# Norm factor in PSUM for VectorE, two weight pairs loaded early into idle gate-output slots, weight loads held for the u stores, and a new order of stages, in an eight-core convolutional decoder

## Chip, cores, metric

One Trainium2 chip, a program on all 8 cores. The time is the device time of the slowest core, in microseconds (us). Executions fall into a fast and a slow state (in the slow one a die runs longer at a lower granted clock); only fast runs are compared here. "Profiled core" is the slowest core of the profiled run; where a number is a median over the eight cores of a trace, the text says so.

## The reference

Two layers, each with an RMSNorm, one input projection, a Conformer convolution branch (A), a short gated convolution branch (B), one output projection and a residual add; a last RMSNorm gives the output. Cut to what matters:

```python
def rmsnorm(x, g):
    xf = x.astype(jnp.float32)
    xn = xf * lax.rsqrt(jnp.mean(xf * xf, axis=-1, keepdims=True) + RMS_EPS)
    return xn.astype(x.dtype) * g
...
    h = rmsnorm(x, norm_g)
    p = jnp.einsum('btd,de->bte', h, w_in)                           # (B, T, D_IN)
...
    u = a_val * jax.nn.sigmoid(a_gate)                               # GLU
    ca, new_a = causal_dwconv(u, buf_a, conv_a_w)
    ca = head_layernorm(ca + conv_a_b, ln_a_g, ln_a_b)
    y_a = jax.nn.silu(ca) * jax.nn.silu(z_a)
    v = gc * hb
    cb, new_b = causal_dwconv(v, buf_b, conv_b_w)
    y_b = gb * cb * jax.nn.silu(z_b)
    y = jnp.einsum('bte,ed->btd', jnp.concatenate([y_a, y_b], axis=-1), w_out)
    return x + y, new_a, new_b
...   # trunk: both layers, then
    return rmsnorm(x, final_g), jnp.stack(new_as, axis=0), jnp.stack(new_bs, axis=0)
```

Each core has one prompt of 2048 tokens and 64 sample tokens, in blocks of 512, 512, 512, 512 and 64 columns.

## The kernel before

The kernel records operations with their data dependences and lets its own list scheduler put them in order on each engine. A stage is a token of the order string: P = one pair of GLU projections (u), C = one convolution, a and b = short-convolution projections, Z = the gate path of A, O4 = a round of the output projection over four finished gate outputs. The second string is the second layer's. Of the transfers, the u stores (`su0`, `su1`) write a finished u to DRAM, and `up` reads it back in the layout that the convolution needs; `toep` holds the weights of a convolution as VectorE lays them out.

```python
ORDER = [
    "b0 C0 Z0 P2 C1 a1 b1 P3 C2 P4 Z1 O4 C3 P5 a2 Z2 b2 Z3 C4 a3 P6 b3 O4 C5 Z4 P7 a4 b4 C6 Z5 a5 b5 C7 Z6 a6 b6u0 a7 Z7u1 b7up",
    "b0 C0 Z0 P2 C1 a1 b1 P3 C2 P4 Z1 O4 C3 P5 a2 Z2 b2 Z3 C4 a3 P6 b3 C5 Z4 P7 O4 a4 b4 C6 Z5 a5 b5 C7 Z6 a6 b6u0 a7 Z7u1 b7up",
]
...
    def rms_stat(part, fill=None, fill_n=(), pool=False, after=(), early=False):
        q, off, n = part
        b = V("bank", "stat")
        ...   # ScalarE squares two chunks, VectorE or GpSimd adds, TensorE sums with a ones matrix into bank b
        r = V("tmp")
        ...
        lo = act((lambda e: e.activation(out=tm(r, n), in_=bank(b, n), func=AF.Ln, bias=RMS_EPS)), n, [b], [r], tab="ln",
                 name=f"rln{q}")
        ...
        ex = act((lambda e: e.activation(out=tm(r, n), in_=tm(r, n), func=AF.Exp, scale=-0.5)), n, [r], [r], sbuf=True, tab="ln",
                 name=f"rex{q}")
        lo.follow = ex
        return r

    def rms_apply(gcol0, part, r, final=False, shared=()):
        ...
            if k in shared:     # final stage only: chunks 2, 5 and 7
                S.op("pool", (lambda e, k=k: e.tensor_tensor(out=xs(k, part), in0=xs(k, part), in1=tm(r, n), op=ALU.mult)), 0.15 + n * 0.0021,
                     [xp(k, part), r], [xp(k, part)], name=f"h{q}.{k}")
            else:               # the "h multiply"
                dve((lambda e, k=k, out=out: e.scalar_tensor_tensor(
                    out=out, in0=xs(k, part), scalar=vecs[:, gcol0 + k:gcol0 + k + 1], in1=tm(r, n), op0=ALU.mult, op1=ALU.mult)),
                    n, [xp(k, part), r, vecs_r], [xp(k, part) if final else h_r[k][q]], ptr=1, name=f"h{q}.{k}")
            ...                 # final: store each pair of chunks (SyncE)
```

```python
    # the scheduler: a load issued by GpSimd waits until the "up" transfers in flight are done
                if e == "pool" and o.chan is not None and t > QUIET:
                    small = {x for x in flying if x.done is None}
                    if small:
                        held.setdefault(o, set()).update(small)
                        skipped.append(it)
                        continue
...
            if o.chan in ("up",):
                flying[:] = [x for x in flying if x.done is None] + [o]
...
    # weights: nine slots of 128 x 1024 in wsl; y_sb has five slots for gate outputs
    def proj(w, q, split=1, **kw):
        ...
            pairs = [((lambda k=k: wsl[:, w.slot, k * 128:(k + 1) * 128]), (lambda k=k: hv(k, q))) for k in ks]
...
    # output projection, layer boundary and end: for each part eight output groups, the statistics of that part,
    # and the h multiplies of the part before
        for part in order:
            for m in range(KC):
                out_block(part, m, lhs, ws + tps, ys)
            r = rms_stat(part, pool=part is not order[-1])
            if before:
                rms_apply(gcol0, *before, final, shared)
```

## Time and profile before

Three runs: 1133.47, 1134.51 and 1342.2 us (the last slow); median 1134.51, from which the prediction starts. From the matmul records of all eight cores I cut the span into stretches, each from the start of one named matmul to the start of the next (the last but one to the end of its matmul); medians of the eight cores:

| stretch (us) | before |
|---|---|
| start to last startup statistic | 66.2 |
| on to the first boundary statistic ("first layer") | 455.5 |
| boundary, first to last statistic | 58.2 |
| second layer | 481.3 |
| first statistic of the output to the last projection matmul ("final projection") | 54.2 |
| after the last projection matmul ("tail") | 13.2 |

How to read it: TensorE works almost without a break in the two long stretches, so only the start, the boundary and the end, and single late weights in the first layer, can give time. The profile lines behind this are in the prediction.

### The profile page before, as it was taken

The page shows a single profiled execution, that of the slowest core. Times are in us where ns is not written, and L with a number is a line of the kernel's source. Part 1 is how long each engine was busy: PE and PEld are TensorE (multiplying, and loading weights), DVE is VectorE, ACT ScalarE, POOL GpSimd, SP SyncE. Part 2 cuts the span into 40 slices and gives each one's busy share as a digit, 9 for nine tenths or more (in the row PEclk, how much of TensorE's full clock was granted, in tenths as well). Part 3 has the DMA queues.
Part 4 walks back from the last instruction along what each step waited for, and adds up shares of the span by engine and source line. Part 5 has one row for each costly group of instructions (what it writes and reads, how often), then busy time and mean ns, then how long its engine had stood idle before and what let it go on. Part 6 is the DMA issues. An engine that isn't in the chain of part 4 may idle for free.

```text
span 1133.5 us, 20988 instructions; the slowest of 8 cores (1126.1 to 1133.5 us)
## 1 busy us (share of the span) xinstructions
PE 1094.8 (97%) x7085; PEld 544.0 (48%) x7085; DVE 780.5 (69%) x1576; ACT 445.5 (39%) x704; POOL 272.6 (24%) x418
## 2 busy tenths in 40 slices
PE   5998999999999999999999999999999999999995
PEld 2444545455445455444444455545545445544444
DVE  3773956897677677754774586687876758774577
ACT  4752334324421443543342144333453223553444
POOL 6120212121202121104451122102211111110286
PEclk9999999999999999999999999999999999999998
DMA  9838689558655757661021876856756633564034
GB/s 217 213 69 136 98 140 161 85 83 113 119 86 85 127 80 113 102 103 20 1 42 14 158 138 109 156 94 120 122 92 117 130 52 66 98 95 101 11 132 165
DMA packets 178823, 117.98 MB, mean 104 GB/s; under 512 B 139168, under 2 KB 152352, under 8 KB 178656
## 3 DMA queue, kind: packets, MB, share of 16 engines
q0 software_dynamic: 34352, 54.97, 33.0%
q1 hardware_dynamic: 144224, 61.65, 24.2%
q8 instruction: 59, 0.97, 0.4%
q14 instruction: 44, 0.36, 0.1%
q10 hardware_dynamic: 144, 0.03, 0.0%
HBM read 132.24 MB, written 36.19 MB: 149 GB/s over the span
## 4 chain that ended last, share of the span: by engine, by line
PE 88%; DMA 4%; POOL 3%; DVE 2%; ACT 2%; issue 2%; DVEq 0%; ACTq 0%; POOLq 0%; SPq 0%
PE psb L584 84%; DMA wsl<-w_in_r 2%; PE psb L757 2%; PE psb L759 2%; DVE h_sb L680 1%; DMA big<-scr_c 1%; DMA scr_c<-big 1%; POOL x_sb L677 1%; DVE x_sb L903 1%; POOL tmp L642 0%; POOL tmp L649 0%; ACT tmp L640 0%; ACT tmp L659 0%; ACT tmp L664 0%; ACT L659 0%
## 5 line engine op out<-in xcount | busy, mean ns | idle before, releaser
L584 PE MATMUL psb<-h_sb,wsl 128*128 128x512 bf16 (+1 forms) x4480 | 823.7, 343 | 7.5 <-DMA wsl<-w_in_r 4.7
L584 PEld LDWEIGHTS psb<-h_sb,wsl 128*128 128x128 bf16 x4480 | 373.2, 98 | 414.8 <-issue 17.8
L584 PE MATMUL psb<-y_sb,wsl 128*128 128x512 bf16 (+2 forms) x992 | 187.1, 336 | 2.4 <-DVE x_sb L903 2.4
L903 DVE TENSOR_TENSOR x_sb<-x_sb,psb 128x512 f32<-128x512 f32 (+2 forms) x248 | 135.5, 575 | 43.5 <-PE psb L584 42.4
L575 POOL DMA_DIRECT2D wsl<-w_in_r x112 | 60.4, 548 | 313.5 <-PE psb L584 206.6
L584 PEld LDWEIGHTS psb<-y_sb,wsl 128*128 128x128 bf16 x992 | 85.1, 98 | 88.5 <-issue 2.6
L884 DVE SCALAR_TENSOR_TENSOR tmp<-vbuf,cw_b_sb,tmp 128x512 f32<-128x512 bf16 (+1 forms) x160 | 103.0, 655 | 23.9 <-ACT tmp L881 11.6
L698 DVE SCALAR_TENSOR_TENSOR u_sb<-tmp,psb 128x512 bf16<-128x512 f32 (+1 forms) x80 | 47.2, 591 | 61.0 <-PE psb L584 52.6
L735 DVE COPY toep<-wt_sb 32x512 bf16<-32x512 bf16 x256 | 74.7, 293 | 20.2 <-DMA wt_sb<-wt_d 9.1
L729 POOL DMA_DIRECT2D wt_sb<-wt_d x64 | 35.0, 547 | 218.8 <-DVE toep L735 124.6
L640 ACT ACTIVATE tmp<-x_sb 128x1024 bf16<-128x1024 f32 (+2 forms) x63 | 52.7, 857 | 85.7 <-DVE x_sb L903 70.0
L854 DVE TENSOR_TENSOR vbuf<-psb,tmp 128x512 bf16<-128x512 f32 (+1 forms) x80 | 47.3, 595 | 56.6 <-PE psb L584 55.8
L696 ACT ACTIVATE tmp<-psb 128x512 f32<-128x512 f32 (+1 forms) x80 | 41.4, 522 | 110.1 <-PE psb L584 108.1
L889 ACT ACTIVATE tmp<-psb 128x512 f32<-128x512 f32 (+1 forms) x80 | 41.6, 522 | 105.2 <-PE psb L584 89.3
L838 ACT ACTIVATE tmp<-big,vecs_sb 128x512 f32<-128x512 bf16 (+1 forms) x80 | 55.7, 731 | 53.0 <-DMA big<-scr_c 46.9
L852 ACT ACTIVATE tmp<-psb 128x512 f32<-128x512 f32 (+1 forms) x80 | 41.4, 521 | 87.7 <-PE psb L584 81.9
L881 ACT ACTIVATE tmp<-vbuf,cw_b_sb 128x512 f32<-128x512 bf16 (+1 forms) x80 | 51.2, 643 | 61.6 <-DVE vbuf L854 57.0
L764 DVE TENSOR_TENSOR big<-psb,cbt_sb 128x320 bf16<-128x320 f32 x128 | 62.4, 487 | 16.8 <-PE psb L759 12.6
L891 DVE TENSOR_TENSOR tmp<-psb,tmp 128x512 f32<-128x512 f32 (+1 forms) x80 | 47.0, 594 | 33.6 <-PE psb L584 31.3
L843 ACT ACTIVATE tmp<-psb 128x512 f32<-128x512 f32 (+1 forms) x80 | 40.6, 520 | 72.0 <-PE psb L584 60.7
L680 DVE SCALAR_TENSOR_TENSOR h_sb<-x_sb,vecs_sb,tmp 128x512 bf16<-128x512 f32 (+1 forms) x80 | 54.9, 742 | 19.7 <-ACT tmp L664 19.7
L844 DVE TENSOR_TENSOR y_sb<-tmp 128x512 bf16<-128x512 f32 (+1 forms) x70 | 41.5, 600 | 21.1 <-ACT tmp L843 20.6
(75 smaller groups left out, 893.8 us busy)
## 6 DMA issues: line engine op xcount, KB each, us to landing
wsl<-w_in_r POOLq DMA_DIRECT2D x112, 256.0 KB, 6.7
scr_u<-u_sb SPq DMA_DIRECT2D x16, 768.0 KB, 8.4
up_sb<-scr_u SPq DMA_DIRECT2D x16, 768.0 KB, 8.4
scr_c<-big SPq DMA_DIRECT2D x16, 640.0 KB, 6.7
big<-scr_c SPq DMA_DIRECT2D x16, 640.0 KB, 6.0
wt_sb<-wt_d POOLq DMA_DIRECT2D x64, 128.0 KB, 3.5
x_sb<-x_d POOLq DMA_DIRECT2D x12, 512.0 KB, 20.2
wsl<-w_out_r POOLq DMA_DIRECT2D x24, 256.0 KB, 6.8
```

The costliest lines, as they stand in the source:

```text
L575: return e.dma_start(out=wsl[:, v.slot, :], in_=src)
L584: ins = e.matmul(bank(v, n), lhsT=l_(), rhs=r_(), start=(first and i == 0), stop=(last and i == len(pairs) - 1))
L640: act((lambda e, s=s, kp=kp: e.activation(out=tmph[:, s.slot, 0:2 * n].rearrange("p (k c) -> p k c", k=2), in_=x2(kp, part), func=AF.Square)),
L680: dve((lambda e, k=k, out=out: e.scalar_tensor_tensor(out=out, in0=xs(k, part), scalar=vecs[:, gcol0 + k:gcol0 + k + 1], in1=tm(r, n), op0 ...
L698: dve((lambda e: e.scalar_tensor_tensor(out=u_blk(ub, q), in0=b3(tm(th, n), q), scalar=1.0, in1=b3(bank(bv, n), q), op0=ALU.add, op1=ALU.m ...
L735: dve((lambda e, p=p, c=c: e.tensor_copy(toep[p, tp.slot, :].rearrange("p (m x) -> p m x", x=128)[:, :, 32 * c:32 * c + 32], wt_sb[p, w.sl ...
L764: dve((lambda e, b=b, v=v, bias=bias: e.tensor_tensor(out=big[:, co.slot, 4 * b:4 * b + 4, :], in0=banks[v.slot][:, 0:384].rearrange("p (g ...
L838: act((lambda e, s=s, q=q, n=n: e.activation(out=b3(tm(s, n), q), in_=c_blk(cn.slot, q), func=AF.Silu, scale=vecs[:, 16 + col:17 + col], b ...
L854: dve((lambda e: e.tensor_tensor(out=v_blk(q, 0), in0=b3(bank(bh, n), q), in1=b3(tm(th, n), q), op=ALU.mult)), n, [bh, th], [v_r[q]], name ...
L881: act((lambda e, a=a, q=q, n=n: e.activation(out=b3(tm(a, n), q), in_=v_blk(q, 0), func=AF.Copy, scale=cw_b[:, l, j, 2:3])), n, [v_r[q], c ...
L884: dve((lambda e, a=a, q=q, n=n, lag=lag: e.scalar_tensor_tensor(out=b3(tm(a, n), q), in0=v_blk(q, lag), scalar=cw_b[:, l, j, 2 - lag:3 - l ...
L903: dve((lambda e: e.tensor_tensor(out=xs(m, part), in0=xs(m, part), in1=bank(v, n), op=ALU.add)), n, [v, xr], [xr], name=f"x{q}.{m}")
```

## The change

The intent: (1) VectorE's h multiply reads the norm factor from PSUM and so doesn't share SBUF reads with GpSimd; (2) the weights of P2 and a1 need no weight slot and come early; (3) weight loads stay out of the way of the u stores (`su0` and `su1` in the diff); (4) an order of stages that fits this. A `lock` flag lets the scheduler model the SBUF port that VectorE and GpSimd share (see the prediction); `FIRST` groups the first blocks one by one, which changes nothing. The diff, cut to its core:

```diff
 ORDER = [
-    "b0 C0 Z0 P2 C1 a1 b1 P3 C2 P4 Z1 O4 C3 P5 a2 Z2 b2 Z3 C4 a3 P6 b3 O4 C5 Z4 P7 a4 b4 C6 Z5 a5 b5 C7 Z6 a6 b6u0 a7 Z7u1 b7up",
-    "b0 C0 Z0 P2 C1 a1 b1 P3 C2 P4 Z1 O4 C3 P5 a2 Z2 b2 Z3 C4 a3 P6 b3 C5 Z4 P7 O4 a4 b4 C6 Z5 a5 b5 C7 Z6 a6 b6u0 a7 Z7u1 b7up",
+    "b0 C0 Z0 P2 a1 b1 C1 P3 C2 P4 Z1 O4 C3 P5 a2 Z2 b2 P6 Z3 C4 a3 b3 O4 a4 C5 P7 Z4 C6 b4 Z5 a5 b5 C7 a6 Z6 b6u0 a7 Z7u1 b7up",
+    "b0 C0 Z0 P2 a1 b1 C1 P3 C2 P4 Z1 O4 C3 P5 a2 Z2 b2 P6 Z3 C4 a3 b3 O4 a4 C5 P7 Z4 C6 b4 Z5 a5 b5 C7 a6 Z6 b6u0 a7 Z7u1 b7up",
 ]
+YW = ("P2", "a1")
...
-            if o.chan in ("up",):
+            if o.chan in ("up", "su0", "su1"):
...
+    def w_pair(tok, srcs):
+        if tok not in YW:
+            return [w_load(src) for src in srcs]
+        v = V("y")
+        ws = [YWeight(v, i) for i in range(2)]
+        for w, src in zip(ws, srcs):
+            nload[0] += 1
+            pooldma((lambda e, w=w, src=src: e.dma_start(out=y_sb[:, v.slot, 1024 * w.half:1024 * w.half + 1024], in_=src)),
+                    1.4, (), [w], f"w{nload[0] % 12}", pkt=0.173, holds=[v], name="w", after=gate)
+        return ws
...
-        ex = act((lambda e: e.activation(out=tm(r, n), in_=tm(r, n), func=AF.Exp, scale=-0.5)), n, [r], [r], sbuf=True, tab="ln",
+        ex = act((lambda e: e.activation(out=bank(b, n), in_=tm(r, n), func=AF.Exp, scale=-0.5)), n, [r], [b], sbuf=True, tab="ln",
                  name=f"rex{q}")
         lo.follow = ex
-        return r
+        if copy:
+            ex.follow = act((lambda e: e.activation(out=tm(r, n), in_=tm(r, n), func=AF.Exp, scale=-0.5)), n, [r], [r], sbuf=True, tab="ln",
+                            name=f"rex{q}")
+        return b, r
...
-                    out=out, in0=xs(k, part), scalar=vecs[:, gcol0 + k:gcol0 + k + 1], in1=tm(r, n), op0=ALU.mult, op1=ALU.mult)),
+                    out=out, in0=xs(k, part), scalar=vecs[:, gcol0 + k:gcol0 + k + 1], in1=bank(r, n), op0=ALU.mult, op1=ALU.mult)),
```

## The prediction

> **What bounds the kernel now.** I read the page first: busy shares and the forty slices.
>
> ```profile
> span 1133.5 us, 20988 instructions; the slowest of 8 cores (1126.1 to 1133.5 us)
> ...
> PE 1094.8 (97%) x7085; PEld 544.0 (48%) x7085; DVE 780.5 (69%) x1576; ACT 445.5 (39%) x704; POOL 272.6 (24%) x418
> ```
>
> TensorE has work in flight for 97% of the span, so the change cannot gain more than about 38.7 us (1133.5 - 1094.8), plus whatever TensorE loses inside its busy time to a halved clock. Nothing in the diff removes a matmul. So the question is where those 38.7 us lie. I asked for busy time by stretch; the columns are length, then PE, PEld, DVE, ACT, POOL, granted clock, DMA share and GB/s:
>
> ```profile
> 0.00:60.00 60.00, 45.45 (x236) 21.30 (x237) 33.05 (x67) 37.12 (x46) 23.91 (x40) 0.97 0.87 205
> 60.00:110.00 50.00, 46.41 (x282) 21.88 (x280) 24.66 (x63) 15.46 (x30) 9.35 (x19) 0.97 0.57 106
> 110.00:530.00 420.00, 419.43 (x2789) 209.22 (x2788) 301.78 (x616) 160.71 (x259) 78.78 (x139) 1.00 0.66 103
> 530.00:590.00 60.00, 55.16 (x305) 25.44 (x304) 46.13 (x76) 25.73 (x34) 32.99 (x30) 0.97 0.11 15
> 590.00:1070.00 480.00, 480.00 (x3198) 239.08 (x3197) 326.67 (x687) 176.76 (x294) 84.12 (x155) 1.00 0.56 99
> 1070.00:1134.00 64.00, 48.32 (x284) 27.10 (x281) 48.25 (x72) 29.70 (x44) 43.42 (x37) 0.91 0.36 136
> ```
>
> TensorE idles 14.6 us while the first x blocks arrive, 3.6 us just after, 0.6 us in the whole middle of layer 0, 4.8 us at the boundary of the layers (the output projection with its RMSNorm statistics), nothing in the middle of layer 1, and 15.7 us at the end. A better order in the middles can gain nothing; it can only break something. Next, TensorE's waits, asked for 60 to 520, 520 to 600 and 1060 to 1134 us in turn:
>
> ```profile
> PE psb L584 <- DMA wsl<-w_in_r: 3.6, 1, 3.6
> ...
> PE psb L584 <- POOL tmp L649: 2.4, 2, 2.0
> PE psb L584 <- DVE x_sb L903: 2.4, 2, 2.0
> ...
> PE psb L584 <- DVE tmp L642: 3.9, 3, 3.2
> PE psb L584 <- POOL tmp L649: 3.1, 3, 1.5
> ```
>
> The first is one weight that came late, until 88.9 us. The others are the square sums (L642, L649) and the residual adds (L903), all made on VectorE and GpSimd. Why those are late, the timeline of 546 to 560 us shows: two h multiplies (L680) that cover 3.26 us, while the GpSimd adds run.
>
> ```profile
> 550.56 1.15 POOL L642 TENSOR_TENSOR tmp<-tmp 128x512 bf16<-128x512 bf16 x1 [3.46 <-ACT tmp L640]
> 550.56 3.26 DVE L680 SCALAR_TENSOR_TENSOR h_sb<-x_sb,vecs_sb,tmp 128x512 bf16<-128x512 f32 x2
> 551.85 1.42 POOL L649 TENSOR_TENSOR tmp<-tmp 128x512 bf16<-128x512 bf16 x1
> 553.74 0.67 DVE L903 TENSOR_TENSOR x_sb<-x_sb,psb 128x512 f32<-128x512 f32 x1
> ```
>
> And the groups by shape (busy us, mean ns):
>
> ```profile
> L903 DVE TENSOR_TENSOR x_sb<-x_sb,psb 128x512 f32<-128x512 f32 x184 | 122.3, 683 | 40.2 <-PE psb L584 39.3
> L680 DVE SCALAR_TENSOR_TENSOR h_sb<-x_sb,vecs_sb,tmp 128x512 bf16<-128x512 f32 x64 | 51.6, 858 | 18.0 <-ACT tmp L664 18.0
> L680 DVE SCALAR_TENSOR_TENSOR x_sb<-x_sb,vecs_sb,tmp 128x512 f32<-128x512 f32 x15 | 20.6, 1402 | 2.1 <-ACT tmp L664 2.0
> L680 DVE SCALAR_TENSOR_TENSOR x_sb<-x_sb,vecs_sb,tmp 128x256 f32<-128x256 f32 x10 | 6.7, 726 | 0.9 <-ACT tmp L664 0.9
> ```
>
> L903 has one SBUF input and one from PSUM, and takes 683 ns wherever it stands. L680 has two SBUF inputs and the same size. In the startup, where GpSimd only issues DMAs, eight of them take 5.39 us (0.67 us each), so 4 x 5.4 = 21.6 us of its 51.6 us are there; the 32 at the boundary get the other 30 us, 0.94 us each. In the final stage they take 1.40 us, twice the uncontended time.
>
> **What the Trainium skill says.** "SBUF — State Buffer", section "Who interferes with whom": a VectorE instruction with two SBUF inputs contends with a GpSimd instruction that reads SBUF, and one with at most one SBUF input, outside the two-port modes, does not; the second to issue waits for the whole of the first. The trace agrees: L680 (two) stretches to 1.40 us, L903 (one) stays at 683 ns. "PSUM — Partial Sum Buffer", the text on engine access, allows one tensor input from PSUM per VectorE instruction, which is what the new form has, and says that GpSimd cannot access PSUM; hence the diff's copy of the factor for the multiplies that the final stage gives to GpSimd. "TensorE: Matmul & The Clock Gate", Part 1: after an idle window of some 3.4 us the clock is halved, and recovers after about 3.4 us of work. The trace agrees: after the 3.6 us gap at 85 us the granted clock of 89 to 95 us is 0.74, and after the gaps at 573 us it is 0.61 in 576 to 580 us.
>
> **The change, part by part.**
>
> (1) The factor in PSUM. The exponential now writes the statistics bank and L680 reads it there. I price the new form by L903, 0.68 us, against 0.67 us uncontended: nothing gained or lost at the start. At the boundary 32 x (0.94 - 0.68) = 8 us of VectorE time go. Per block of 512 VectorE then needs 8 adds + 8 multiplies = 16 x 0.68 = 10.9 us against TensorE's 64 x 0.2155 = 13.8 us, so the adds keep up; now they do not (VectorE is busy 5.0 of 5 us in 571 to 576). I expect the 4.8 us of waits there to go, and with them the halved clock behind: the first two groups of eight matmuls take 2.6 and 2.5 us instead of 1.73, 1.6 us together. Sum 6.4 us.
>
> At the end, 15 x (1.40 - 0.68) + 10 x (0.73 - 0.41) = 14 us of VectorE time go (0.41 us is the 256-wide L903). GpSimd's multiplies, up to 1.72 us against 1.27, shorten too. TensorE's waits between 1080 and 1120 us, 0.8 + 0.8 + 1.5 = 3.1 us, should go. Behind TensorE's last projection matmul (ends 1120.3) 13.2 us follow now. Priced without contention: add 0.45, square 0.65, sum 0.3, matmul 0.3, Ln 0.38, Exp 0.42, second Exp for GpSimd 0.42, three GpSimd multiplies 2.3, store about 3.3 (issue and a median landing of 2.4), and 0.1 us for each of eight hand-overs: 9.3 us. So 3.9 us more. Sum 7.0 us. The extra Exp is on an engine that is 39% busy and costs 0.42 us once, counted here.
>
> (2) Early weights. The 3.6 us wait was for the third projection pair (P2), which had no free weight slot before 75.6 us and then flew with five more weights and two u stores (landing 13.5 us median, 6.7 over the run). In the order of the changed kernel the four weights of P2 and a1 are issued in the startup, behind the x loads in the same queue, into idle y slots, some 50 us before use; from 60 to 76 us the DMA engines moved nothing. Gain 3.6 us, plus 6 us x 0.26 = 1.5 us of lost clock in 89 to 95 us. Sum 5.1 us. Layer 1 gets the same, but had no wait there.
>
> (3) Weight loads wait for u stores too. That shortens 16 stores (8.4 us median), whose readers TensorE does not wait for, and delays weight loads by up to as much. Each pair feeds TensorE for 64 x 0.2155 + 16 x 0.03 = 14.3 us, and nine slots hold some four pairs, so such a delay should be hidden. Gain 0, risk 0 to 4 us.
>
> (4) The new order of the stages. The first convolution comes 24 matmuls earlier, and layer 0 becomes like layer 1. No gain to be had; risk 0 to 3 us. The grouping of the first blocks changes nothing, since every group has one block; the lock flag only steers the scheduler.
>
> Sum: 6.4 + 7.0 + 5.1 = 18.5 us, so 1134.5 - 18.5 = 1116.0 with nothing given back. I add 3.5 us for waits that take the place of removed ones, which gives 1119.5 us (-1.3%).
>
> **The rivals.** (a) The statistics wait, not the multiply, sets the boundary: the bank is now held until the multiplies are done, there are two such banks, and the square sums still go through two GpSimd adds (1.15 us each). For it: the PE order still places the second statistics matmul three output groups (5.2 us) behind the block, and add + square + two adds need about 4.4 us; thin. Against: the multiplies end before the bank after next is wanted. Half the gain at boundary and end would go: about 1126. (b) The middles break: a weight held behind a u store, or a convolution that meets its load. For it: the first u stores land only at 85 to 89 us in the trace, and P2's first u must wait for one. Against: without the weights beside them they should land sooner. 1122 to 1127. (c) The trace's waits are all there is and a better start also speeds the rest, giving more than 2% (below 1111.8): it would need 22.7 us, more than my full sum. (d) The early weights delay the x loads: they stand behind them in the queue, so I give it little; 1130.
>
> **Range and chances.** All removed and nothing new is 1116; half given back is 1125. Below 1112 there is little left to take, since the first 14.6 us of startup wait for x. Range 1113 to 1128; faster by over 2% 0.08, within 2% 0.91, slower by over 2% 0.01.
>
> **What would show it.** The h multiply at about 0.68 us at the boundary and in the final stage; no wait of TensorE for a weight after 60 us; boundary waits under 1.5 us; about 9 us behind the last projection matmul; the middles still without waits. It would be wrong if TensorE idles over 3 us in the middles, if the boundary keeps its waits for L649's successor, or if the PSUM form takes clearly more than 0.7 us.

## The result, and the profile after

The changed kernel takes 1122.91 us, the median of four runs (1121.54 to 1123.34), against 1134.33 us, the median of the three fast runs of the kernel before beside it (a fourth was slow). The ratio is 0.9899, 95% interval 0.988 to 0.9919. (A ratio is the mean time of one kernel's fast runs over that of the other's in the same rounds, so it isn't quite the ratio of the quoted medians.)

The head of its page, and the stretches (columns as in the prediction), answer to those of before:

```profile
span 1121.6 us, 20982 instructions; the slowest of 8 cores (1117.3 to 1121.6 us)
...
PE 1091.3 (97%) x7085; PEld 544.6 (49%) x7085; DVE 759.2 (68%) x1576; ACT 444.6 (40%) x709; POOL 265.5 (24%) x418
```

```profile
60.00:110.00 50.00, 49.60 (x343) 24.77 (x343) 32.17 (x81) 17.53 (x35) 9.54 (x19) 1.00 0.50 109
...
530.00:590.00 60.00, 59.83 (x337) 28.20 (x336) 44.57 (x92) 25.57 (x36) 32.63 (x34) 1.00 0.28 40
...
1060.00:1122.00 62.00, 46.54 (x281) 27.21 (x278) 35.21 (x71) 31.47 (x48) 36.53 (x37) 0.90 0.37 140
```

TensorE's idle time after the startup fell from 3.6 to 0.4 us, that of the boundary from 4.8 to 0.2 us, and the granted clock is 1.00 in both. The last stretch still has 15.5 us (62.00 - 46.54). TensorE's waits, asked for 60 to 520, 520 to 600 and 1060 to 1122 us (waited for: us in total, times, longest):

```profile
PE psb L616 <- DVE h_sb L719: 0.4, 1, 0.4
...
PE psb L616 <- DVE x_sb L942: 0.2, 1, 0.2
...
PE psb L616 <- DVE tmp L676: 1.8, 2, 1.1
```

No weight is waited for, and no GpSimd add. Between 600 and 1060 us there is no wait at all. The groups by shape (L942 is the residual add, L903 before; L719 the h multiply, L680 before):

```profile
L942 DVE TENSOR_TENSOR x_sb<-x_sb,psb 128x512 f32<-128x512 f32 x184 | 124.1, 686 | 49.1 <-PE psb L616 48.1
L719 DVE SCALAR_TENSOR_TENSOR h_sb<-x_sb,vecs_sb,psb 128x512 bf16<-128x512 f32 x64 | 44.1, 743 | 13.7 <-ACT psb L699 13.7
L719 DVE SCALAR_TENSOR_TENSOR x_sb<-x_sb,vecs_sb,psb 128x512 f32<-128x512 f32 x15 | 10.7, 743 | 1.9 <-ACT psb L699 1.8
...
L719 DVE SCALAR_TENSOR_TENSOR x_sb<-x_sb,vecs_sb,psb 128x256 f32<-128x256 f32 x10 | 4.2, 475 | 0.8 <-ACT psb L699 0.8
```

The multiply of the final stage fell from 1402 to 743 ns, and that of 128x256 from 726 to 475 ns. At the boundary, the mean of the 32 multiplies of 128x512 fell from 957 to 744 ns, counted one by one in the traces. The timeline of the boundary shows the pair of multiplies that covered 3.26 us, now beside a GpSimd add as then:

```profile
549.20 1.15 POOL L676 TENSOR_TENSOR tmp<-tmp 128x512 bf16<-128x512 bf16 x1 [0.88 <-ACT tmp L674]
...
549.37 1.40 DVE L719 SCALAR_TENSOR_TENSOR h_sb<-x_sb,vecs_sb,psb 128x512 bf16<-128x512 f32 x2
```

Two multiplies take 1.40 us, and the add its 1.15 us. So the first part does what it is meant to. Now the stretches, medians of the eight cores:

| stretch (us) | before | after | difference | predicted |
|---|---|---|---|---|
| first layer | 455.54 | 453.04 | -2.5 | -5.1 |
| boundary | 58.19 | 52.36 | -5.8 | -6.4 |
| second layer | 481.31 | 481.38 | +0.1 | 0 |
| final projection | 54.15 | 50.24 | -3.9 | -3.1 |
| tail | 13.19 | 15.91 | **+2.7** | -3.9 |

The tail grew, though the multiplies in it became shorter. The instructions of the block end tell why. A DRAIN stands after the engine's last instruction and is issued while that one may still wait or run, so its length alone says little. What counts is when it ends: in all fourteen traces VectorE's ends 0.05 us after the engine's last instruction, ScalarE's 0.04 and TensorE's 0.05 us, but GpSimd's 2.37 or 9.31 us. First the kernel before (engine, operation, count: ns minimum/median/maximum, first and last start in us; the q marks the engine's sequencer):

```profile
L1062 POOLq DRAIN  x1: 4774/4774/4774, 1126.5 to 1126.5; - x1
L1062 DVEq DRAIN  x1: 3447/3447/3447, 1126.6 to 1126.6; - x1
L1062 SPq DRAIN  x1: 7/7/7, 1133.3 to 1133.3; - x1
```

And the changed kernel:

```profile
L1104 DVEq DRAIN  x1: 1580/1580/1580, 1110.0 to 1110.0; - x1
L1104 POOLq DRAIN  x1: 11359/11359/11359, 1110.0 to 1110.0; - x1
L1104 SPq DRAIN  x1: 7/7/7, 1115.2 to 1115.2; - x1
```

And GpSimd's last three multiplies, in the kernel before and in the changed one:

```profile
1126.44 2.44 POOL L677 TENSOR_TENSOR x_sb<-x_sb,tmp 128x256 f32<-128x256 f32 x3 [2.01 <-ACT tmp L664]
```

```profile
1110.01 2.09 POOL L716 TENSOR_TENSOR x_sb<-x_sb,tmp 128x256 f32<-128x256 f32 x3 [2.24 <-ACT tmp L703]
```

SyncE's DRAIN comes after its wait for the last store, so all outputs have landed by 1115.2 us. But the span ends at 1121.6 us. GpSimd's DRAIN, issued at 1110.0 us, lasts 11.4 us (to 1121.4) where it lasted 4.8. SyncE's waits near the end, before and then after:

```profile
SPq L1062 <- PEq L1062: 0.2, 1, 0.2
```

```profile
SPq L1104 <- PEq L1104: 6.4, 1, 6.4
```

PEq only passes the barrier on: the view names who signalled last, and PE in turn had waited for the others. GpSimd's own signal is at 1121.5 us, just after its DRAIN. Measured from the end of GpSimd's last multiply, the DRAIN ends 2.37 us later in the kernel before and 9.31 us later in the changed one, on every one of the eight cores. It gives some 6.3 us of the gain back (15.91 - 9.64 us, the tail with the long and with the short drain in the runs below).

### The profile page after: what moved, and what is told of

The parts are those of the page before. It is cut to its first block, busy times and chain, and to the rows that moved or that the text cites. A ratio compares the mean times of both kernels' runs of the same rounds, so it can differ in the third digit from the quotient of the medians.

```text
span 1121.6 us, 20982 instructions; the slowest of 8 cores (1117.3 to 1121.6 us)
## 1 busy us (share of the span) xinstructions
PE 1091.3 (97%) x7085; PEld 544.6 (49%) x7085; DVE 759.2 (68%) x1576; ACT 444.6 (40%) x709; POOL 265.5 (24%) x418
## 4 chain that ended last, share of the span: by engine, by line
PE 95%; DMA 1%; POOL 1%; ACT 1%; DVE 0%; issue 0%; POOLq 0%; ACTq 0%; DVEq 0%
PE psb L616 92%; PE psb L796 2%; PE psb L798 2%; DMA wsl<-w_in_r 1%; POOL toep L1014 0%; ACT L693 0%; POOL wsl L583 0%; POOL x_sb L983 0%; POOL u_sb L1003 0%; ACT psb L699 0%; ACT tmp L693 0%; DVE h_sb L719 0%; POOL x_sb L716 0%; DVE tmp L676 0%; ACT L735 0%
## 5 line engine op out<-in xcount | busy, mean ns | idle before, releaser
L616 PE MATMUL psb<-h_sb,wsl 128*128 128x512 bf16 (+1 forms) x4160 | 762.9, 343 | 3.8 <-DVE h_sb L719 2.2
L616 PEld LDWEIGHTS psb<-h_sb,wsl 128*128 128x128 bf16 x4160 | 347.2, 98 | 381.8 <-issue 9.9
L942 DVE TENSOR_TENSOR x_sb<-x_sb,psb 128x512 f32<-128x512 f32 (+2 forms) x248 | 137.2, 578 | 53.6 <-PE psb L616 52.6
L583 POOL DMA_DIRECT2D wsl<-w_in_r x104 | 56.0, 546 | 283.7 <-PE psb L616 207.4
L616 PE MATMUL psb<-h_sb,y_sb 128*128 128x512 bf16 (+1 forms) x320 | 58.9, 342 | 0.0
```

The costliest lines, as they stand in the source:

```text
L583: return e.dma_start(out=wsl[:, v.slot, :], in_=src)
L616: ins = e.matmul(bank(v, n), lhsT=l_(), rhs=r_(), start=(first and i == 0), stop=(last and i == len(pairs) - 1))
L942: dve((lambda e: e.tensor_tensor(out=xs(m, part), in0=xs(m, part), in1=bank(v, n), op=ALU.add)), n, [v, xr], [xr], name=f"x{q}.{m}")
```

## The experiments

Theory at the start: the PSUM factor gives the boundary and the end, the early weights the first layer, and some side effect of the change on GpSimd's DRAIN takes some 6.3 us back. Rivals: the long drain comes with the PSUM factor itself; or one of the other parts costs time somewhere. Twelve kernels ran; times are medians of their own fast runs, ratios are against the fast runs of the kernel before in the same job. All twelve gave correct results. For orientation, the results (stretches in us, medians of eight cores; drain = end of GpSimd's DRAIN after its last multiply):

| kernel | time | ratio, 95% interval | first layer | tail | drain |
|---|---|---|---|---|---|
| before | 1134.33 | 1 | 455.54 | 13.19 | 2.37 |
| after | 1122.91 | 0.9899 [0.988, 0.9919] | 453.04 | 15.91 | 9.31 |
| psum_only | 1121.49 | 0.9891 [0.9875, 0.9906] | 455.30 | 9.65 | 2.37 |
| yw_only | 1130.92 | 0.9978 [0.996, 0.9996] | 453.24 | 13.19 | 2.37 |
| no_psum | 1135.10 | 1.0016 [0.9998, 1.0034] | 453.10 | 18.12 | 9.31 |
| pad24 | 1123.31 | 0.9906 [0.9888, 0.9924] | 453.13 | 15.91 | 9.31 |
| after_v48 | 1122.85 | 0.9904 [0.9884, 0.9924] | 453.17 | 15.91 | 9.31 |
| psum_v5 | 1122.81 | 0.9902 [0.9882, 0.9923] | 456.59 | 9.93 | 2.37 |
| old_order | 1120.28 | 0.9878 [0.9854, 0.9901] | 454.36 | 9.64 | 2.37 |
| no_yw | 1127.88 | 0.994 [0.9922, 0.9958] | 457.90 | 15.91 | 9.31 |
| mix_new_old | 1116.52 | 0.9842 [0.9819, 0.9865] | 453.15 | 9.64 | 2.37 |
| no_last_share | 1118.08 and 1119.33 | none | 453.14 | 11.59 | 9.31 |
| pool_late8 | 1122.49 | 0.9893 [0.9873, 0.9914] | 453.10 | 15.91 | 9.31 |
| pool_pad1 | 1124.03 | 0.99 [0.9884, 0.9915] | 453.21 | 15.91 | 9.31 |

### psum_only: the kernel before with the factor in PSUM alone

The edit is the last two hunks of the diff above, applied to the kernel before.

> The kernel before with the norm factor in PSUM and nothing else. Theory A (the port is the cause of the boundary and end waits): the boundary stretch (first to last statistics matmul there, median of the cores 58.2 us before, 52.4 in the changed kernel) falls to about 52.4, the final projection stretch from 54.15 to about 50.2, the first layer stays at some 455.5; the time falls by about 9.7 us before the tail behind the last projection matmul is counted. Theory B (the order and the scheduler's new knowledge of the port do it): the boundary stays over 56 us and the time changes by less than 4 us. Tail: 9 to 10 us (time about 1120.6) if its growth to 15.9 us in the changed kernel has nothing to do with the PSUM form, 15.9 us (about 1127.5) if it comes with it.

Measured: 1121.49 us, as fast as the whole change. Boundary 52.38 us, final projection 50.24 us, as in the changed kernel; the tail is 9.65 us. Its drain:

```profile
L1066 POOLq DRAIN  x1: 4421/4421/4421, 1113.1 to 1113.1; - x1
L1066 SPq DRAIN  x1: 7/7/7, 1118.4 to 1118.4; - x1
```

So the PSUM factor gives the boundary and the final stretch by itself, and does not bring the long drain.

### yw_only: the kernel before with the early weights alone

```diff
+YW = ("P2", "a1")
-                wg, wv = w_load(w_in_r[l, 8 + j]), w_load(w_in_r[l, j])
+                wg, wv = w_pair(tok, (w_in_r[l, 8 + j], w_in_r[l, j]))
...   # with YWeight, w_pair, w_ap and the gate of the change
```

> The kernel before with the early weights of P2 and a1 alone. Theory: only the wait of TensorE for a weight behind the startup goes, so the first layer's stretch falls from 455.5 us (median of the cores) to about 453 and the time by 2 to 4 us, to about 1132; boundary, second layer and end as before. Rival: the early loads delay the x blocks in the same queue, the startup (58.7 us) grows by over 1 us and nothing is gained.

Measured: 1130.92 us. The first layer takes 453.2 to 453.3 us on every core, where the kernel before had 454.3 to 459.3; its TensorE has no wait left between 60 and 520 us. The startup did not grow (65.8 against 66.2 us), so the rival falls. The drain is short, the tail unchanged. This is all that the change reaches in the first layer (453.0), without its order, its hold and its lock flag.

### no_psum: the changed kernel with the factor in SBUF

```diff
-        ex = act((lambda e: e.activation(out=bank(b, n), in_=tm(r, n), func=AF.Exp, scale=-0.5)), n, [r], [b], ...
+        ex = act((lambda e: e.activation(out=tm(r, n), in_=tm(r, n), func=AF.Exp, scale=-0.5)), n, [r], [r], ...
-        ... in1=bank(r, n), op0=ALU.mult, op1=ALU.mult)),
+        ... in1=tm(r, n), op0=ALU.mult, op1=ALU.mult)),
```

> The changed kernel with the factor in SBUF again and all the rest kept. Theory A: boundary back to about 58 us and the final projection to about 54 us, so about 9.7 us slower before the tail; with the tail of the kernel before (13.2 us) 1130 us. Theory B (order, early weights and store holds carry the gain): within 3 us of 1122.9.

Measured: 1135.10 us, the median of three fast runs, no gain over the kernel before. Boundary 58.34 and final projection 54.14 us are back at the old values, and the tail is 18.12 us: the slow multiplies and the long drain together, 4.9 us more than the expectation of 1130 us allowed for. So the long drain belongs to what remains of the change: early weights, hold, order, lock.

### pad24: 24 one-element memsets on GpSimd

The idea was that the length of GpSimd's instruction stream sets the drain, by where it ends in a block of fetched instructions.

```diff
+    pad = sb("pad", [128, 64], F32)
                 for n_o, o in enumerate(self.order[name]):
+                    if name == "pool" and n_o == 240:
+                        for i_ in range(24):
+                            e.memset(Sched.pad[:, i_:i_ + 1], 0.0)
```

> The changed kernel with 24 one-element memsets on GpSimd early in layer 1, which shift its instruction stream by 24 and nothing else. The last instruction of GpSimd in the changed kernel ends 9.3 us behind its last multiply, 2.4 us in the kernel before. Theory F (an instruction fetch falls there, and where it falls depends on the number of instructions): the tail falls from 15.9 to about 9.0 us and the time to about 1116. Rival D (the long end belongs to the new form of the tail itself): tail 15.9 us, time 1122.9.

Measured: nothing moved (tail 15.91 us). The memsets stand at 627 us in the trace, early in the second layer. That theory falls for GpSimd's stream.

### after_v48 and psum_v5: memsets on VectorE

In the traces with the long drain a fetch of instructions fell near the end, and it kept step with VectorE's count of instructions. So the theory was turned to VectorE's stream: 48 memsets more in the changed kernel should move the fetch away, five more in psum_only should bring it in. The edit is that of pad24 with `name == "dve" and n_o == 700`.

> The changed kernel with 48 one-element memsets on VectorE put into the middle of the first layer, where TensorE has no waits. It computes the same. The changed kernel loses about 6.5 us at the very end, in which GpSimd's last drain takes 9.3 us in place of 2.4 us, and in those runs a fetch of VectorE's instructions falls near the end; the runs with the long drain recorded 3262 or 3263 VectorE instructions, those with the short one 3257 to 3259. Theory F (the length of VectorE's instruction stream decides): with 48 more the fetch comes some 48 instructions before the end, the drain is short again, the stretch after the last projection matmul goes from 15.9 to about 9.5 us, and the time from 1122.9 to about 1116.5 us. Rival O (something else of the changed kernel, such as its order of stages or its waits, decides): the stretch stays at 15.9 us and the time at 1122.9 us within 1 us. The memsets themselves cost at most 1 us in either case.

> The kernel before with the norm factor in PSUM alone, and five one-element memsets on VectorE in the middle of the first layer, so that it records 3264 VectorE instructions in place of 3259. Theory F (length of VectorE's instruction stream): the stretch after the last projection matmul goes from 9.7 to about 16 us, and the time from 1121.5 to about 1128 us. Rival O: 9.7 us and 1121.5 us, as without the memsets.

Measured: the fetch moved as foreseen and the drain didn't. The DMA view from 1105 to 1122 us (queue: packets, MB, share), first the changed kernel with 48 memsets, long drain and no fetch:

```profile
q1 hardware_dynamic: 2191, 2.13, 37.1%
```

Then psum_only with five, short drain and a fetch (queue 14):

```profile
q1 hardware_dynamic: 2722, 4.07, 65.7%
q14 instruction: 1, 0.01, 0.2%
```

The theory of the fetch falls both ways. (psum_v5 is 1.3 us above psum_only, from another job, and so is its first layer, 456.6 against 455.3 us, in which it still waits for late weights. Its tail is 0.28 us longer, nothing like the 6.3 us of the long drain.)

### old_order: the changed kernel with the order of before

```diff
 ORDER = [   # both strings as in the kernel before
```

> The changed kernel with the order of stages of the kernel before; everything else as changed. If the first layer's gain comes from the early weights and not from the order: the time from the last startup statistic to the first boundary statistic stays at 453.0 to 453.6 us (453.04 changed, 455.54 before), and the second layer at 481.4. If the order gave it: about 455. The tail tells of the long drain: if the order of stages brings it (rival O), the stretch after the last projection matmul is about 9.5 us here and the whole about 1116.5 to 1117 us; if not, about 16 us and 1123 us.

Measured: 1120.28 us, tail 9.64 us, drain 2.37 us. So the order of stages brings the long drain. The first layer takes 454.36 us here (453.9 to 457.5 by core), between the two expectations: the new order is worth some 1.3 us in it, given the rest of the change. It is no gain over the kernel before: yw_only has the old order and the early weights, and its first layer takes 453.24 us. old_order differs from it by the hold, the lock flag and the PSUM factor, and the last changed nothing there in psum_only (455.30 against 455.54 us). So the hold or the lock flag seems to cost the old order about 1.1 us, and the new order only makes that good. The slowest core of the profiled run (1118.61 us) spent 457.5 us in its first layer, which fits a time above the expected 1116.5 to 1117 us.

### no_yw: the changed kernel without the early weights

```diff
-YW = ("P2", "a1")
+YW = ()
```

> The changed kernel without the early weights: no stage loads its weights into gate-output slots. If the early weights give the first layer's gain: the time from the last startup statistic to the first boundary statistic goes from 453.0 back to about 455.5 us and, with the weights again awaited on some cores (454.3 to 459.3 in the kernel before), the time from 1122.9 to about 1125.5 to 1128 us if the long drain stays, 6.5 us less if it goes. If the changed order hides the weights by itself: 453 us and no difference apart from the drain.

Measured: 1127.88 us, 5.0 us above after_v48 in the same job, which runs like the changed kernel. The first layer takes 457.9 us. TensorE waits between 60 and 520 us:

```profile
PE psb L616 <- DMA wsl<-w_in_r: 4.5, 2, 2.5
PE psb L796 <- DVE toep L774: 1.2, 1, 1.2
```

The new order without the early weights is worse than the old one (457.9 against 455.5 us): it needs them. With them, they are worth 4.9 us.

### mix_new_old, no_last_share and pool_late8: which layer, and is it the drain?

```diff
 ORDER = [   # mix_new_old: first string new, second as in the kernel before
-SHARED = {p: (2, 5, 7) for p in LASTP[1:]}
+SHARED = {p: (2, 5, 7) for p in LASTP[1:-1]}      # no_last_share
+                    if name == "pool" and n_o == len(self.order[name]) - 3:      # pool_late8
+                        for i_ in range(8):
+                            e.memset(Sched.pad[:, i_:i_ + 1], 0.0)
```

> The changed kernel with its own order of stages in the first layer and the order of the kernel before in the second. Five kernels with the changed order in both layers had the 9.3 us drain of GpSimd at the end, five with the order of before in both had the 2.4 us drain. If what the second layer leaves on GpSimd decides the drain (theory G): the drain is 2.4 us, the stretch after the last projection matmul about 9.6 us, and with the first layer's 453.0 us kept the time is 1116 to 1117 us, the fastest of all. If the first layer's order decides it (or the length of something counted over the whole run): 15.9 us and 1122.9 us. The second layer itself (481.3 us) should not move in either case by more than 0.5 us.

Measured: 1116.52 us, the fastest of all, the median of three fast runs from 1115.63 to 1118.00 (a fourth was slow). pool_late8, which runs like the changed kernel, took 1122.49 us in the same job. First layer 453.15 us as in the changed kernel, second layer 481.24, tail 9.64. Head of its page, and its drain:

```profile
span 1116.3 us, 20995 instructions; the slowest of 8 cores (1111.8 to 1116.3 us)
```

```profile
L1104 POOLq DRAIN  x1: 4419/4419/4419, 1111.0 to 1111.0; - x1
L1104 SPq DRAIN  x1: 7/7/7, 1116.1 to 1116.1; - x1
```

Outputs landed at 1116.1 and the span ends at 1116.3 us. So the second layer's order brings the long drain, and without it nothing follows the last store.

> The changed kernel in which GpSimd takes no multiplies of the last part of the output, so that its last instruction ends some 4.3 us earlier; VectorE does 3 more multiplies of 475 ns, 1.4 us, in the last part. If GpSimd's drain is what gives the gain back, and it stays at 9.3 us: it then ends some 5 us before the outputs have landed plus nothing else to wait for, or about with them, and the stretch after the last projection matmul goes from 15.9 to 10.5 to 12 us and the time from 1122.9 to about 1118 to 1119 us. If the long drain is only a sign of something else that ends late (an instruction fetch, a barrier between engines), taking GpSimd away leaves 15.9 us or adds the 1.4 us of VectorE: 1123 to 1124.5 us.

Measured: the fast runs are 1118.08 and 1119.33 us (two more were slow, so there is no interval), against 1122.49 us for pool_late8 in the same job, and the tail is 11.59 us. Its drain, and SyncE's wait at the end:

```profile
L1104 POOLq DRAIN  x1: 11454/11454/11454, 1104.8 to 1104.8; - x1
```

```profile
SPq L1104 <- PEq L1104: 1.3, 1, 1.3
```

The drain is as long, but GpSimd started it earlier, so the end comes earlier although VectorE has three more multiplies. This is the causal test: the end follows GpSimd's drain. A drain that is long by a fixed amount can be hidden by letting that engine finish first.

> The changed kernel with eight one-element memsets on GpSimd just ahead of its last three multiplies, where it idles for 2.1 us; they cost nothing on the path to the end. If the drain's length depends on which kinds of instruction GpSimd ran last (theory G in its near form): the drain may change from 9.3 us, to 2.4 us or another length, and the time with it (1116.4 us at 2.4 us). If it is set earlier than that, or by something outside GpSimd's instructions: 9.3 us, 15.9 us after the last projection matmul, 1122.9 us.

Measured: 1122.49 us, drain 9.31 us. A different kind of instruction just ahead of its last three doesn't shorten it.

### pool_pad1: one memset on GpSimd

In all traces so far the recorded number of GpSimd instructions had been even with the short drain and odd with the long one, and the earlier insertions had been of even numbers. One more run could decide that.

```diff
                         # as pad24, with range(1)
```

> The changed kernel with a single one-element memset more on GpSimd, in the middle of the first layer. In the thirteen kernels traced so far the recorded number of GpSimd's instructions is even (794, 796, 802) in all six with the 2.4 us drain and odd (791, 795, 797, 803, 819) in all seven with the 9.3 us drain; the earlier insertions on GpSimd were of 24 and 8 memsets and left it odd. Theory N (whether the number is even or odd decides, and the order of stages matters only through the number of waits that it makes): with 796 the drain is 2.4 us, the stretch after the last projection matmul 9.6 us in place of 15.9, and the time about 1116.5 us (1115.5 to 1117.5). Theory G (the second layer's order itself decides, by what it leaves on GpSimd): 9.3 us, 15.9 us and 1122.9 us, as with 8 and with 24 memsets.

Measured: 1124.03 us, 796 instructions recorded, an even number, and drain 9.31 us. Even or odd was chance.

## Why the prediction was right, and where a step of it failed

The time (1122.91 us) lies in the range 1113 to 1128 and within 2%, 3.4 us above the predicted 1119.5. Its mechanism for the gain, the operand moved to PSUM, is shown; its end of the program is not what happened. By its own steps:

**The factor in PSUM, at the boundary: right.** Predicted -6.4, measured -5.8 us as the median of the cores (58.19 to 52.36) and -6.8 between the profiled cores (59.2 to 52.4). The multiply is at 0.70 us in the pair shown, beside GpSimd adds, TensorE's boundary waits are 0.2 us and the clock is not halved. psum_only shows that this part alone does it, and no_psum that nothing else does. Two readings under it were off. The price of 0.68 us mixed two measures: one multiply takes 743 ns in every stage now, and took 747 ns (median, at the start) undisturbed before, while 0.67 us is the distance between multiplies that follow each other (5.36 us for eight at the start now, 5.39 before). So the 32 multiplies gave back 32 x (0.957 - 0.744) = 6.8 us of VectorE time, not 8. And of the two gaps in which the prediction finds the idle window of 3.4 us, only the one at 85 us (3.59 us) is that long: the gaps at 573 us were of 2.0 and 0.4 us, and the clock was halved for 3.41 us all the same.

**The end: right for what was added up, wrong for what was left out.** The final projection gave 3.9 us, against 3.1. The tail was priced at 9.3 us; where the drain is short, it is 9.65, 9.64, 9.64 and 9.93 us (psum_only, old_order, mix_new_old, psum_v5). But in the changed kernel it is 15.9. The step that failed is the sum "So 3.9 us more": it followed the arithmetic up to the last store and its landing, and took for granted that the span ends there. In the profile of before, GpSimd's DRAIN ended at 1131.3 us (1126.5 + 4.8), 2.0 us ahead of SyncE's at 1133.3, and so was not seen. The second layer's new order made the drain 6.9 us longer (9.31 - 2.37), which used up that lead (0.7 us in mix_new_old, with its faster multiplies) and more; the step neither named a DRAIN nor asked what an order of stages could do to one.

**Waits that take the place of removed ones: right as an allowance, wrong in kind.** 3.5 us were added, for no named wait; 6.3 us came (15.91 - 9.64). That the allowance covered over half of it is luck. With the allowance at zero the prediction was 1116.0 us, and the kernel without the long drain, mix_new_old, takes 1116.52. None of the four rivals is what happened. (a) fell with the 0.2 us at the boundary; (b) with the middles free of waits, though no_yw shows that the new order does break the first layer (weights 4.5 us, toep 1.2 us) where it has no early weights; (c) asked for more than the full sum; (d) with startup statistics that took no longer (66.2 before, 65.8 us after, medians over the cores).

**The early weights: the right mechanism, and a size that was read from one core.** No weight is waited for. The 5.1 us came from core 7, the profiled one, and on core 7 the first layer did shrink by 6.3 us (459.3 to 453.0). But the wait was of 0.9 to 3.6 us over the eight cores, and the median gain is 2.5 us. The slowest core after is another, core 5, which starts 2.2 us later than core 7 did before. The difference of the two profiled cores adds up: +2.2 start, -6.2 first layer, -6.8 boundary, +0.2 second layer, -3.9 final projection, +2.7 tail, in all -11.9 us before rounding (1133.49 to 1121.64). So this part gave about 4.0 us of the time together with the later start, and 3.1 us when alone (yw_only, 1130.92 against 1134.06 us for the fast runs of the kernel before in its job).

**The hold for the u stores and the order: not as harmless as priced, but elsewhere.** The second layer moved by 0.1 us. The new order in the first layer gains about 1.3 us beside the hold and the lock flag (old_order), where 0 was predicted, but nothing over the early weights alone (yw_only, 453.24 us against 453.04); in the second layer it costs 6.0 us through the drain (1122.49 for pool_late8 to 1116.52 us for mix_new_old, in one job). No run has the hold or the lock flag alone, so their shares stay open.

**What stays open** is why GpSimd's drain is 2.37 or 9.31 us. Shown: it is the same on all eight cores, it goes with the second layer's order of stages, and it does not depend on the PSUM factor, the early weights, the instruction fetch near the end, the memsets added to GpSimd's or VectorE's stream (1, 8 or 24, and 5 or 48), an even or odd count, or which multiplies GpSimd runs last. The hold and the lock flag do not bring the long drain by themselves (old_order has both). GpSimd's streams differ in many places of the second layer. The last of them is some 115 to 135 us before the end: in all eight traces with the long drain three copies alternate there with weight issues, and in all six with the short one they follow them in a row. No run tested that.

## What to carry to other kernels

Price a tail up to the end of the program, not to the last store: look at the block end's DRAIN of each engine, and keep the engine with the long one away from the last work. Give VectorE's operand from PSUM where GpSimd adds run beside it. Read a wait on all cores before you count it: the time is that of the slowest core, and taking a wait from one core can make another the slowest.

## What the Trainium skill lacked or had wrong

- "VectorE: DVE Perf Modes", section "The DRAIN you can't avoid", knows, besides the flush after each VectorE instruction, only boilerplate DRAINs of about 12 ns on all five engines. Here the DRAIN at the block end took 7 ns on SyncE, but about 0.4 us on ScalarE, 1.6 to 3.4 us on VectorE, and 4.4 to 11.7 us on GpSimd. On ScalarE and VectorE nearly all of that is the engine's own unfinished work (they end 0.04 and 0.05 us after it); on GpSimd 2.37 or 9.31 us come on top, and in the changed kernel they set the end of the program.
- No page says that GpSimd's DRAIN has two lengths for the same last instructions: it ended 2.37 us after its last multiply in six of the fourteen kernels traced and 9.31 us in eight, by the order of stages in the second layer.
- "Runtime: NRT & Kernel Launch", section "Instruction fetch mechanics", gives blocks of 16 KiB for the refill of an engine's instructions. The trace has them on one queue (59 packets, 0.97 MB) and packets of half that on another (45 packets, 0.37 MB, some 8 KB each). That section calls a crossing "mostly hidden", which agrees within 0.3 us: the tail is 15.91 us with a fetch in it and without (changed kernel, after_v48), and 9.93 us with one against 9.65 us without (psum_v5, psum_only).
